# A hybrid decoder step on one core: attention scores as two full 128-row matmuls, and RWKV's triangular inverse with T and A·T side by side in one PSUM bank

## The chip, the cores and the metric

One core of one Trainium2 chip runs the whole program in one launch. The metric is the device time of that launch in microseconds (us). TensorE (PE) does the matmuls, VectorE (DVE), ScalarE (ACT) and GpSimd (POOL) do the elementwise work, and 16 DMA engines move data; every engine works through its own list of instructions in order and waits on semaphores for the others.

## The reference

One layer of a decoder: a combined input projection feeds four groups of heads, whose gated outputs go through one output projection. Two of the groups matter here.

```python
# group A, differential attention: 4 heads, two softmax maps (c) per head, 64 numbers per query and key
s = jnp.einsum('bqhcd,bkhcd->bhcqk', q, k) * (DQK ** -0.5)      # + ALiBi bias, causal
pr = jax.nn.softmax(s + bias)
w = pr[:, :, 0] - lam * pr[:, :, 1]
...
# group B, RWKV-7: 8 heads of 64, 1024 steps, a state s of 64x64 per head
def step(s, inp):
    sa = jnp.einsum('bhvk,bhk->bhv', s, a_t)
    s = s * w_t[:, :, None, :] + sa[..., None] * b_t[:, :, None, :] + v_t[..., None] * k_t[:, :, None, :]
    return s, jnp.einsum('bhvk,bhk->bhv', s, r_t)
```

The kernel computes group B in chunks of 64 steps. Inside a chunk the rows `sa` depend on each other through a strictly triangular 64x64 matrix A, so that each head and chunk needs the triangular inverse T = (I - A)^-1.

## The kernel before

**The projections.** `Kern.block` (line 562) computes x @ w as a stream of matmuls with 128 rows, 128 columns of weights and 344 tokens: each product is made of three fp32r matmuls (high·high, high·low, low·high), as operands are split into a high and a low part (`split_piece`, lines 538 and 539: ACT makes `whi`, DVE `wlo`). There are 9,936 of these and 96 more in `block_dt`; every other stage is woven into this stream.

**The weaving.** `Driver.run` holds generators ("lanes"), each a stage of the model. A lane runs until it yields a number, the microseconds of model time after which it wants to go on; in between the driver emits matmuls of the projection, 8 at a time, and each adds 344/2400 us to the model clock `K.now`. So the order of the work on PE is set by the program, ahead of time, from these numbers; the operations of the small matmuls add to the clock as well (`K.mm`, `K.tp`, and a line in `mixer_a`). The Tile layer then orders each engine's list and adds the semaphores.

**Attention** (`mixer_a`, one head after the other). Keys and queries come from DRAM as `k2` and `q2`: for each map c the 64 rows stand twice, on partitions 0 to 63 and 64 to 127. ACT rounds the keys to fp32r (`kh`) and DVE makes the remainder `kl` on 64 partitions; `qs` holds the rounded queries on 64 partitions and their remainder on the other 64. For each block i of 128 queries and each piece of up to 512 keys, `scores` issues two matmuls per map (lines 1507 and 1508): `qs` x `kh` over 128 rows gives (high + low query)·high key, and `qs` x `kl` over 64 rows adds high query·low key. Then one DVE instruction (line 1511) adds the bias and takes the maximum, ACT does the exponential (line 1518) and DVE normalises (lines 1521, 1522). Scores use a pool of three PSUM banks; the scores of block i + 1 are issued ahead of the transposes `p_wt` and the products `p_o` of block i.

**RWKV** (`Rwkv`, three lanes). `elements` prepares the operands of a unit (2 blocks of two heads, 128 steps: J = 4 matrices for each half of the partitions, 16 units in all), `products` does the matmuls, `norm` the output. For each unit `products` does:

- `p_gram`: 8 matmuls give the 64x64 matrices; ACT copies A to `at` (line 926), DVE masks the rest (`gs`, line 936);
- the inverse by doubling: T starts with blocks of 2 on its diagonal, four levels double them to 32, and a last step joins two of 32. T is kept with its transpose in `tm`. A level l (0 to 3) takes two rounds through PE: `p_w` = A_l · T (8 matmuls of 64 rows, 64 columns, 64 wide), DVE adds the identity (`wpl`, line 949), `p_t` = that times T (8 matmuls); then ACT copies `p_t` to `tm` (line 972) and DVE transposes it (line 973). DVE also masks the next level's A (`nl`, line 963). The last step works on quarters of 32x32 (two `p_w` groups, lines 983 to 991);
- `p_bt`: transposes of `bk`; then for each half c of the unit `p_z`, `p_y` (products with the state S), `p_sa` (T times z), `p_s` and `p_y` (update of the state and output), each ended by small copies on DVE and ACT.

A small f32 matmul shows as two records in the trace; the 8 matmuls of a level are 16 records. `products` yields 0.8 and 0.7 between the two rounds of a level.

Of the kernel before, what the change touches and what calls it, by code (L numbers as in the profile page):

```python
# [45 lines left out]
def constants():  # L46

    p = np.arange(128)
    s = p % 64
    t = np.arange(64)  # L50
    c = {}
    c["ident"] = np.eye(128)
    strict = (t[None, :] > s[:, None])
    incl = (t[None, :] >= s[:, None])
    c["gmask"] = np.concatenate([strict, incl], 1)
    lm = []
    for n in (1, 2, 4, 8, 16):
# [7 lines left out]
    c["mt"] = np.concatenate([x[1] for x in lm[1:]], 1)  # L65
    c["bones"] = (p[:, None] // 64 == p[None, :] // 64)
# [64 lines left out]
class Kern:  # L131
# [46 lines left out]
    def mm(self, out, lhsT, rhs, start, stop):  # L178
# [5 lines left out]
        self.nc.tensor.matmul(out, lhsT=lhsT, rhs=rhs, start=start, stop=stop)  # L184
# [643 lines left out]
class Rwkv:  # L828
# [16 lines left out]
    TWO = ("nl", "tm", "rn", "gst4", "bon128")  # L845
# [56 lines left out]
    def products(self):  # L902
# [7 lines left out]
        for it in range(self.UNITS):  # L910
# [17 lines left out]
            tm = P.tile([128, 2, J, 64], F32, name="tm", tag="tm")  # L928
            nc.vector.tensor_tensor(tm[:, 1], at, m1, op=ALU.mult)
            nc.vector.tensor_tensor(tm[:, 1], tm[:, 1], e64.to_broadcast([128, J, 64]), op=ALU.add)  # L930
            flat = lambda x: x.rearrange("p j t -> p (j t)")
            nc.vector.transpose(flat(tm[:, 0]), flat(tm[:, 1]))  # L932
            nl = P.tile([128, J, 64], F32, name="nl", tag="nl")
            nc.vector.tensor_tensor(nl, at, mt[:, 0].unsqueeze(1).to_broadcast([128, J, 64]), op=ALU.mult)
            for h in range(2):
                nc.vector.tensor_tensor(gs[:, h], pg[h], gm, op=ALU.mult)

            yield 2.3
            sav = P.tile([128, J, 2, 64], F32, name="sav", tag="sav")
            s4 = sav.rearrange("p (b c) h t -> p b c h t", c=2)  # L940
            for l in range(4):
                pw = ps("p_w")
                pwv = pw[:, :J * 64].rearrange("p (j t) -> p j t", j=J)
                for j in range(J):
                    for h in range(2):
                        q = slice(h * 64, h * 64 + 64)
                        K.mm(pwv[q, j, :], lhsT=nl[q, j, :], rhs=tm[q, 0, j, :], start=True, stop=True)
                wp = P.tile([128, J, 64], F32, name="wpl", tag="nl")
                nc.vector.tensor_tensor(wp, pwv, e64.to_broadcast([128, J, 64]), op=ALU.add)  # L949
                if l == 0:  # L950

                    p = ps("p_v")
                    for b in range(nb):
                        K.tp(p[:, b * 128:b * 128 + 128], v[:, b, :], K.id)
                    pv = p[:, :N].rearrange("p (b h t) -> p b h t", b=nb, h=2)
# [15 lines left out]
                tm = P.tile([128, 2, J, 64], F32, name="tm", tag="tm")  # L971
                nc.scalar.copy(tm[:, 0], ptv)  # L972
                nc.vector.transpose(flat(tm[:, 1]), pt[:, :J * 64])  # L973
                yield 0.7
# [3 lines left out]
            wp = P.tile([128, J, 64], F32, name="wpl", tag="nl")  # L978
            for j in range(J):
                for h in range(0, 128, 64):  # L980
                    u, w = slice(h, h + 32), slice(h + 32, h + 64)
                    K.mm(pwv[w, j, 0:32], lhsT=at[u, j, 32:64], rhs=tm[u, 0, j, 0:32], start=True, stop=True)
            nc.vector.tensor_copy(out=wp[32:64, :, 0:32], in_=pwv[32:64, :, 0:32])
            nc.scalar.copy(wp[96:128, :, 0:32], pwv[96:128, :, 0:32])
            yield 1.05
            for j in range(J):
                for h in range(0, 128, 64):
                    u, w = slice(h, h + 32), slice(h + 32, h + 64)
                    K.mm(pwv[u, j, 32:64], lhsT=wp[w, j, 0:32], rhs=tm[w, 1, j, 32:64], start=True, stop=True)
            nc.vector.tensor_copy(out=tm[0:32, 1, :, 32:64], in_=pwv[0:32, :, 32:64])  # L990
            nc.scalar.copy(tm[64:96, 1, :, 32:64], pwv[64:96, :, 32:64])
            tq = tm[:, 1]

            bt = P.tile([128, J, 2, 64], F32, name="bt", tag="tm")
# [8 lines left out]
            for c in range(2):  # L1003

                pz, py = ps("p_z"), ps("p_y")
                bh = [(b, h, slice(h * 64, h * 64 + 64), slice(64 - h * 64, 128 - h * 64), slice(b * 64, b * 64 + 64))
                      for b in range(nb) for h in range(2)]
                for b, h, q, w, n in bh:
                    K.mm(pz[w, n], lhsT=ar[q, 2 * b + c, 0, :], rhs=S[q, b0 + b, :], start=b == 0, stop=False)
                for b, h, q, w, n in bh:  # L1010
                    K.mm(pz[w, n], lhsT=gs[q, h, 2 * b + c, 0:64], rhs=sav[q, 2 * b + c, h, :], start=False, stop=b == nb - 1)
                for b, h, q, w, n in bh:
                    K.mm(py[q, n], lhsT=ar[q, 2 * b + c, 1, :], rhs=S[q, b0 + b, :], start=b == 0, stop=False)
                z = P.tile([128, nb, 64], F32, name="z", tag="z")
                nc.vector.tensor_copy(out=z.rearrange("p b t -> p (b t)"), in_=pz[:, :nb * 64])
                yield 0.51
# [34 lines left out]
        for a in range(2):  # L1051
            so = P.tile([64, 4, 64], F32, name="sob", tag="nl")
# [407 lines left out]
def mixer_a(K, P):  # L1460
    nc = K.nc
    for h in range(4):
# [6 lines left out]
        q2 = P.tile([128, 2, T], F32, name="aq2", tag="ae", bufs=2)  # L1469
# [8 lines left out]
        qs = P.tile([128, 2, T], F32R, name="aqs", tag="aqs")  # L1478
        kh = P.tile([128, 2, T], F32R, name="akh", tag="akh")
        kl = P.tile([128, T], F32R, name="akl", tag="akl")  # L1480
        nc.scalar.copy(kh, k2)
        yield 0.00
        for c in range(2):
            r = slice(c * 64, c * 64 + 64)
            nc.vector.tensor_tensor(kl[r], k2[r, c, :], kh[r, c, :].bitcast(F32), op=ALU.subtract)
        nc.scalar.copy(qs, q2)
        yield 1.50
        for c in range(2):
            r = slice(64 - c * 64, 128 - c * 64)
            nc.vector.tensor_tensor(qs[r, c, :], q2[r, c, :], qs[r, c, :].bitcast(F32), op=ALU.subtract)  # L1490
        yield 1.00
# [4 lines left out]
        def scores(i):  # L1496
# [3 lines left out]
            npc = (nk + 511) // 512  # L1500
            for pc in range(npc):
                k0, k1 = pc * 512, min(nk, pc * 512 + 512)
                for c in range(2):
                    r = slice(c * 64, c * 64 + 64)
                    p = K.ps("p_s", 0)
                    t = slice(i * 128, i * 128 + 128)
                    nc.tensor.matmul(p[:, :k1 - k0], lhsT=qs[:, c, t], rhs=kh[:, c, k0:k1], start=True, stop=False)
                    nc.tensor.matmul(p[:, :k1 - k0], lhsT=qs[r, c, t], rhs=kl[r, k0:k1], start=False, stop=True)  # L1508
                    K.now += 2 * max(k1 - k0, 256) / 2400
# [612 lines left out]
```

## Time and profile before

| | us |
|---|---|
| median of 3 runs (lowest to highest) | 2227.99 (2224.55 to 2231.98) |
| the profiled execution's own time | 2238.66 |
| its span, first to last instruction | 2236.9 |
| attention on PE, about | 176 to 540 |
| RWKV's products on PE, about | 685 to 1396 |
| granted TensorE clock, mean | 0.995 |

A row of the timeline gives the start of an instruction (or of a run of equal ones, with their count), its duration, engine, line, operation, what it writes and reads, and its shape; an idle time ahead of it stands in brackets with what ended it. Matmuls overlap in the pipeline and their ends are modelled: what one costs PE is read from the distance between starts.

### The profile page before, as it was taken

What the parts mean: (1) busy time and instruction counts of PE and PEld (TensorE: products, weight loads), DVE (VectorE), ACT (ScalarE), POOL (GpSimd) and SP (SyncE); (2) the same over time, 40 slices, a digit from 0 to 9 for tenths busy, and PEclk for the clock granted to TensorE, in tenths of its full rate; (3) what the DMA queues carried; (4) which work ended last, traced back from release to release, by engine and by line L of the source; (5) the groups of instructions that cost most, each with busy time, mean ns of one, the idle gap of its engine ahead of it and who ended that gap; (6) DMA issues with size and microseconds to landing.
All of it is one profiled execution on the core that took longest, in us unless ns stands there. A gap on an engine that the chain in (4) does not pass through costs nothing. (4 is left out here: it accounts for less than half of the span.)

```text
span 2236.9 us, 42918 instructions
## 1 busy us (share of the span) xinstructions
PE 2183.9 (98%) x16964; PEld 2010.3 (90%) x16964; DVE 1189.1 (53%) x2869; ACT 813.1 (36%) x2079; POOL 184.9 (8%) x246
## 2 busy tenths in 40 slices
PE   8999999999999999999999999999999999999997
PEld 6798989899998888889888888899989999999997
DVE  6714353444225567673668875476653544333554
ACT  7724343444222344432344343112211134333544
POOL 2100000000000000020100000350031100000000
PEclk9999999999999999999999999999999999999999
DMA  7652425241322223152322211664565584222791
GB/s 262 192 136 61 133 68 142 67 119 41 112 66 63 68 64 86 57 172 76 107 58 81 66 53 49 183 216 129 150 183 144 160 262 130 79 74 72 223 255 51
DMA packets 320851, 263.50 MB, mean 118 GB/s; under 512 B 29356, under 2 KB 294906, under 8 KB 319952
## 3 DMA queue, kind: packets, MB, share of 16 engines
q1 hardware_dynamic: 307792, 218.92, 34.2%
q0 software_dynamic: 12192, 40.28, 5.8%
q8 instruction: 134, 2.20, 0.4%
q10 hardware_dynamic: 664, 1.54, 0.2%
q14 instruction: 69, 0.57, 0.1%
HBM read 205.93 MB, written 54.80 MB: 117 GB/s over the span
## 5 line engine op out<-in xcount | busy, mean ns | idle before, releaser
L562 PE MATMUL acc<-hh,wlo 128*128 128x344 f32 x3312 | 1079.1, 326 | 6.0 <-DVE wlo L539 3.8
L562 PE MATMUL acc<-hh,whi 128*128 128x344 f32 x3312 | 1076.2, 325 | 6.9 <-ACT whi L538 2.6
L562 PE MATMUL acc<-hl,whi 128*128 128x344 f32 x3312 | 1078.0, 325 | 1.6 <-issue 1.6
L562 PEld LDWEIGHTS acc<-hh,whi 128*128 128x128 f32 x3312 | 624.4, 189 | 17.3 <-ACT whi L538 3.6
L562 PEld LDWEIGHTS acc<-hh,wlo 128*128 128x128 f32 x3312 | 623.1, 188 | 17.3 <-DVE wlo L539 5.9
L562 PEld LDWEIGHTS acc<-hl,whi 128*128 128x128 f32 x3312 | 625.8, 189 | 8.8 <-issue 3.6
L539 DVE TENSOR_TENSOR wlo<-raw,whi 128x512 fp32r<-128x512 f32 x300 | 206.9, 690 | 406.9 <-ACT whi L538 398.1
L538 ACT CAST whi<-raw 128x512 fp32r<-128x512 f32 x300 | 185.4, 618 | 494.1 <-PE acc L562 401.1
L1511 DVE CUSTOM_DVE_ANT_0 ae<-p_s,al 128x512 f32<-128x512 f32 (+3 forms) x96 | 52.9, 557 | 51.0 <-PE p_s L1508 49.9
L1518 ACT ACTIVATE ae<-ae,am 128x128 f32<-128x128 f32 (+7 forms) x64 | 49.2, 771 | 57.6 <-DVE am L1515 57.5
L1832 ACT ACTIVATE p_out<-xo 128x128 f32<-128x128 f32 (+1 forms) x144 | 39.8, 276 | 78.5 <-DVE xo L1831 74.1
L1831 DVE TENSOR_TENSOR xo<-xo,p_out 128x128 f32<-128x128 f32 (+1 forms) x144 | 39.4, 280 | 27.1 <-PE p_out L188 26.9
L972 ACT COPY tm<-p_t 128x256 f32<-128x256 f32 x64 | 23.9, 373 | 74.0 <-PE p_t L184 73.8
L184 PEld LDWEIGHTS p_w<-tm,nl 64*64 64x64 f32 x1024 | 34.9, 134 | 17.5 <-issue 12.9
L539 DVE TENSOR_TENSOR wlo<-oraw,whi 128x512 fp32r<-128x512 f32 x48 | 33.2, 692 | 31.7 <-ACT whi L538 31.4
L184 PEld LDWEIGHTS p_t<-wpl,tm 64*64 64x64 f32 x1024 | 35.0, 134 | 15.4 <-issue 8.6
L184 PE MATMUL p_w<-tm,nl 64*64 64x64 f32 x1024 | 43.6, 224 | 2.7 <-DVE tm L932 2.7
L184 PE MATMUL p_t<-wpl,tm 64*64 64x64 f32 x1024 | 43.9, 224 | 0.5 <-DVE wpl L949 0.5
L214 POOL TENSOR_TENSOR ass<-ass,mhalf 128x8 f32<-128x8 f32 x4 | 6.6, 1643 | 453.4 <-DVE ass L1559 453.4
L1619 POOL DMA_INDIRECT sakp<-in_cache_diff_k,sapt x32 | 40.9, 1278 | 31.3 <-DMA r<-sda 16.7
L973 DVE STREAM_TRANSPOSE tm<-p_t 128x256 f32<-128x256 f32 x64 | 28.5, 446 | 26.8 <-ACT tm L972 26.5
L214 POOL TENSOR_TENSOR osr<-osr,mhalf 128x1 f32<-128x1 f32 (+1 forms) x9 | 6.0, 691 | 443.8 <-DMA xo<-in_x_prompt 319.6
(468 smaller groups left out, 2708.2 us busy)
## 6 DMA issues: line engine op xcount, KB each, us to landing
raw<-in_w_in SPq DMA_DIRECT2D x220, 256.0 KB
raw<-in_w_out SPq DMA_DIRECT2D x80, 256.0 KB
oraw<-in_w_out SPq DMA_DIRECT2D x12, 1024.0 KB
evm<-sm SPq DMA_DIRECT2D x48, 172.0 KB
sB<-evs SPq DMA_DIRECT2D x39, 172.0 KB
sA<-evp SPq DMA_DIRECT2D x36, 172.0 KB
evo<-so SPq DMA_DIRECT2D x36, 172.0 KB
sm<-evo SPq DMA_DIRECT2D x36, 172.0 KB
```

What stands on the lines that cost most here:

```text
L184: self.nc.tensor.matmul(out, lhsT=lhsT, rhs=rhs, start=start, stop=stop)
L214: self.nc.gpsimd.tensor_tensor(out, x, self.mhalf[:P, :n], op=ALU.pow)
L538: nc.scalar.copy(hi, raw)
L539: nc.vector.tensor_tensor(lo, raw, hi.bitcast(F32), op=ALU.subtract)
L562: nc.tensor.matmul(acc[g][:, :G], lhsT=x[:, k, :], rhs=y, start=kp == ko[0] and k == 0 and x is hi and y is a, stop=kp == ko[-1] and k == ...
L972: nc.scalar.copy(tm[:, 0], ptv)
L973: nc.vector.transpose(flat(tm[:, 1]), pt[:, :J * 64])
L1511: nc.vector.tensor_tensor_reduce(e[:, c, k0:k1], p[:, :k1 - k0], al[:, x0:x0 + k1 - k0], 1.0, -3e38, ALU.add, ALU.max, m[:, c, pc:pc + 1])
L1518: nc.scalar.activation(e[:, c, :nk], e[:, c, :nk], AF.Exp, bias=m[:, c, 0:1], accum_out=z[:, c:c + 1])
L1619: nc.gpsimd.indirect_dma_start(out=dst, out_offset=None, in_=I[src].rearrange("a p c -> (a p) c"), in_offset=bass.IndirectOffsetOnAxis(ap= ...
L1831: nc.vector.tensor_tensor(xt, xt, q[:n, k * 128:k * 128 + 128], op=ALU.add)
L1832: nc.scalar.activation(q[:n, k * 128:k * 128 + 128], xt, AF.Square, accum_out=self.ss[:n, 3 * g + k, cb:cb + 1])
```

## The change

In **attention**, keys are kept in one tile `km`: the rounded keys on partitions 0 to 63, their remainder on 64 to 127, for both maps. The queries are made block by block (`queries(i)`, two buffers, one block ahead): `qt` holds the rounded query on both halves of the partitions (a = 0) and the remainder on both (a = 1). A score is then two matmuls over 128 rows, high query and low query against `km`. `q2` lies in a buffer of its own (the one `qs` had) and not in the pair of buffers of `e`.

In **RWKV**, one PSUM bank `p_t` holds T and A·T side by side for a unit, 32 columns of each for every 64 rows (within the levels up to 16, T has 32x32 blocks on its diagonal alone). A first round of 8 matmuls writes both; then a level takes one round: DVE masks A·T out of the bank (`xl`, x), transposes it in SBUF, ACT copies the bank to SBUF (`rt`), and 8 matmuls add the level's correction to T and to A·T in the bank itself, without clearing it; the last of the four adds to T alone. The 8 matmuls have 64 columns each as before, as two runs of 32, in the last round one run of 32. T's transpose is made once, at the end (`tm`), and T is spread to 64 columns (`tq`). The first state products (c = 0) are issued directly behind the last round, ahead of the 32x32 steps. `products` yields 1.2 for each level, and before `p_sa` of c = 0 it no longer yields.

```diff
@@ Rwkv.products
+            xl = P.tile([128, 2, J, 64], F32, name="xl", tag="xl")
+            xm, lt = xl[:, 0], xl[:, 1]
+            nc.vector.tensor_tensor(xm, at, m1, op=ALU.mult)
+            nc.vector.tensor_tensor(xm, xm, e64.to_broadcast([128, J, 64]), op=ALU.add)
+            nc.vector.transpose(flat(lt), flat(xm))
+            rt = P.tile([128, 2, J, 32], F32, name="rt", tag="rt")
+            nc.gpsimd.tensor_copy(out=rt[:, 0], in_=K.c("eye32").unsqueeze(1).to_broadcast([128, J, 32]))
+            for h in range(2):
+                for o in (0, 32):
+                    q = slice(64 - h * 64 + o, 96 - h * 64 + o)
+                    nc.scalar.copy(rt[q, 1], pg[h][q, :, o:o + 32])
...
-                        K.mm(pwv[q, j, :], lhsT=nl[q, j, :], rhs=tm[q, 0, j, :], start=True, stop=True)
-                wp = P.tile([128, J, 64], F32, name="wpl", tag="nl")
-                nc.vector.tensor_tensor(wp, pwv, e64.to_broadcast([128, J, 64]), op=ALU.add)
...
-                        K.mm(ptv[q, j, :], lhsT=tm[q, 1, j, :], rhs=wp[q, j, :], start=True, stop=True)
-                tm = P.tile([128, 2, J, 64], F32, name="tm", tag="tm")
-                nc.scalar.copy(tm[:, 0], ptv)
-                nc.vector.transpose(flat(tm[:, 1]), pt[:, :J * 64])
-                yield 0.7
...
+                    K.mm(ptv[q, :, j, :], lhsT=lt[q, j, :], rhs=rt[q, :, j, :], start=j == 0, stop=j == J - 1)
...
+                nc.vector.tensor_tensor(xm.rearrange("p j (k t) -> p j k t", k=2),
+                                        ptv[:, 1].unsqueeze(2).to_broadcast([128, J, 2, 32]),
+                                        mt[:, l].rearrange("p (k t) -> p k t", k=2).unsqueeze(1).to_broadcast([128, J, 2, 32]),
+                                        op=ALU.mult)
+                nc.vector.transpose(flat(lt), flat(xm))
+                rt = P.tile([128, 2, J, 32], F32, name="rt", tag="rt")
+                n = 2 if l < 3 else 1
+                nc.scalar.copy(rt[:, :n].rearrange("p a j t -> p (a j t)"), pt[:, :n * J * 32])
...
+                yield 1.2
+                        K.mm(ptv[q, :n, j, :], lhsT=lt[q, j, :], rhs=rt[q, :n, j, :], start=False, stop=j == J - 1,
+                             skip_group_check=True)
+            first = state_products(0)
+            tm = P.tile([128, J, 32], F32, name="tm", tag="tm")
+            nc.vector.transpose(flat(tm), pt[:, :J * 32])
+            tq = P.tile([128, J, 64], F32, name="tq", tag="tq")
...
+                z, py = state_products(c) if c else first
+                if c:
+                    yield 0.51
@@ mixer_a
+        km = P.tile([128, 2, T], F32R, name="akm", tag="akh")
+        nc.scalar.copy(km, k2)
+        nc.vector.tensor_tensor(km[64:128], k2[64:128], km[64:128].bitcast(F32), op=ALU.subtract)
+        def queries(i):
+            t = slice(i * 128, i * 128 + 128)
+            qt = P.tile([128, 2, 2, 128], F32R, name="aqt", tag="aqt", bufs=2)
+            nc.scalar.copy(qt[:, 0], q2[:, :, t])
+            nc.vector.tensor_tensor(qt[:, 1], q2[:, :, t], qt[:, 0].bitcast(F32), op=ALU.subtract)
+            return qt
...
-                    nc.tensor.matmul(p[:, :k1 - k0], lhsT=qs[:, c, t], rhs=kh[:, c, k0:k1], start=True, stop=False)
-                    nc.tensor.matmul(p[:, :k1 - k0], lhsT=qs[r, c, t], rhs=kl[r, k0:k1], start=False, stop=True)
-                    K.now += 2 * max(k1 - k0, 256) / 2400
+                    for a in range(2):
+                        nc.tensor.matmul(p[:, :k1 - k0], lhsT=qt[:, a, c], rhs=km[:, c, k0:k1], start=a == 0, stop=a == 1)
+                    K.now += 2 * max(k1 - k0, 128) / 2200
```

The order of the instructions shows three places. The first is PE in attention, the scores of query block 6 of the first head: `p_o` is the product of block 4, `p_s` a bank of scores, `ak..` are keys, `aq..` queries, `acc` the projection. Before:

```order
L184 MATMUL p_o_2429<-av_2021,aw_2408 128x128 x5
L1507 MATMUL p_s_2440<-akh_1983,aqs_1982 128x512
L1508 MATMUL p_s_2440<-akl_1984,aqs_1982 128x512
L1507 MATMUL p_s_2444<-akh_1983,aqs_1982 128x512
L1508 MATMUL p_s_2444<-akl_1984,aqs_1982 128x512
L1507 MATMUL p_s_2448<-akh_1983,aqs_1982 128x384
L1508 MATMUL p_s_2448<-akl_1984,aqs_1982 128x384
```

The same place on PE now:

```order
L186 MATMUL p_o_2433<-av_2018,aw_2415 128x128 x5
L1531 MATMUL p_s_2447<-akm_1982,aqt_2373 128x512 x2
L1531 MATMUL p_s_2451<-akm_1982,aqt_2373 128x512 x2
L1531 MATMUL p_s_2455<-akm_1982,aqt_2373 128x384 x2
L564 MATMUL acc1_2106<-hh_12_1_1106,whi_2318 128x344
L1531 MATMUL p_s_2459<-akm_1982,aqt_2373 128x384 x2
```

The scores stand where they stood, two matmuls to a bank; the pair is now of one kind.

The second place is DVE in the levels of unit 13, with work of another lane (`sst`, `stt`: the sampled tokens' state) between. Before (`wpl`, `nl` and the transposed `tm` are the level's, `p_w` and `p_t` PE's banks):

```order
L949 TENSOR_TENSOR wpl_13853<-p_w_13844,cst2_5645 128x256
L963 TENSOR_TENSOR nl_13855<-at_13732,cst2_5645 128x256
L783 TENSOR_TENSOR kk_13878<-rkv_13798,pt_134 128x256
L1177 TENSOR_TENSOR stt_13687<-svv_12982,svec_12979 128x1024
L973 STREAM_TRANSPOSE tm_13875<-p_t_13866 128x256
L1179 TENSOR_TENSOR sst_13686<-sst_13686,stt_13687 128x1024
L949 TENSOR_TENSOR wpl_13898<-p_w_13889,cst2_5645 128x256
```

DVE in the levels now (`xl` is the masked A·T and its transpose):

```order
L979 TENSOR_TENSOR xl_13477<-p_t_13428,cst2_5739 128x256
L1189 TENSOR_TENSOR stt_13284<-sst_13283,svec_13276 128x1024
L983 STREAM_TRANSPOSE xl_13477<-xl_13477 128x256
L794 TENSOR_REDUCE rn_13554<-ksq_13513 128x4
L1191 TENSOR_REDUCE ssa_13285<-stt_13284 128x16
L979 TENSOR_TENSOR xl_13506<-p_t_13428,cst2_5739 128x256
```

A level has two DVE instructions instead of three, both between two visits of PE, and the other lane's instruction can stand between them.

The third place is PE around the first `p_sa` of a unit. Before (`p_w` is the second 32x32 step, `p_z` and `p_y` the first state products, `p_xs` another lane's):

```order
L184 MATMUL p_w<-tm,wpl 32x32 x8
L188 MATMUL p_bt<-cst_129,bk 128x128 x4
L184 MATMUL p_z<-S,ar 64x64 x4
L184 MATMUL p_z<-sav,gs 64x64 x4
L184 MATMUL p_y<-S,ar 64x64 x4
L184 MATMUL p_bon<-ksq,cst_5645 128x256
L184 MATMUL p_xs<-xmk,xq 128x256 x2
L184 MATMUL p_sa<-z,tm 64x64 x4
```

Now, in another unit (`p_kb` and `p_kn` belong to the operands of later work):

```order
L186 MATMUL p_w<-tq,wpl 32x32 x8
L190 MATMUL p_bt<-cst_129,bk 128x128 x4
L190 MATMUL p_kb<-cst_129,rx 128x128 x2
L186 MATMUL p_kn<-ksq,cst_5739 128x32
L186 MATMUL p_sa<-z,tq 64x64 x4
```

The state products no longer stand between the 32x32 step and `p_sa`. Over the whole program the projection's stream on PE consists of 519 unbroken runs before and of 477 now.

More of the change, by code (lines that the diff above doesn't have):

```diff
@@ L65, in constants @@
     c["mt"] = np.concatenate([x[1] for x in lm[1:]], 1)
+    c["own"] = (s[:, None] // 32 == t[None, :] // 32)
+    c["eye32"] = (p[:, None] % 32 == np.arange(32)[None, :])
     c["bones"] = (p[:, None] // 64 == p[None, :] // 64)
@@ L175, in ps, with mm @@
         return (self.p2 if ring else self.pb).tile([128, 512], F32, name=name, tag="mx")
-    def mm(self, out, lhsT, rhs, start, stop):
+    def mm(self, out, lhsT, rhs, start, stop, **k):
         cols = 1
@@ L183, in mm @@
         self.now += max(0.03, cols * f * 4 / 2400)
-        self.nc.tensor.matmul(out, lhsT=lhsT, rhs=rhs, start=start, stop=stop)
+        self.nc.tensor.matmul(out, lhsT=lhsT, rhs=rhs, start=start, stop=stop, **k)
     def tp(self, out, in_, ident):
@@ new lines, in state_products @@
+            def state_products(c):
+                pz, py = ps("p_z"), ps("p_y")
+                for b, h, q, w, n in bh:
+                    K.mm(pz[w, n], lhsT=ar[q, 2 * b + c, 0, :], rhs=S[q, b0 + b, :], start=b == 0, stop=False)
+                for b, h, q, w, n in bh:
+                    K.mm(pz[w, n], lhsT=gs[q, h, 2 * b + c, 0:64], rhs=sav[q, 2 * b + c, h, :], start=False, stop=b == nb - 1)
+                for b, h, q, w, n in bh:
+                    K.mm(py[q, n], lhsT=ar[q, 2 * b + c, 1, :], rhs=S[q, b0 + b, :], start=b == 0, stop=False)
+                z = P.tile([128, nb, 64], F32, name="z", tag="z")
+                nc.vector.tensor_copy(out=z.rearrange("p b t -> p (b t)"), in_=pz[:, :nb * 64])
+                return z, py
@@ new lines, in products @@
+            yield 2.3
+            pt = ps("p_t")
+            ptv = pt[:, :J * 64].rearrange("p (a j t) -> p a j t", a=2, j=J)
+            for j in range(J):
+                for h in range(2):
+                    q = slice(h * 64, h * 64 + 64)
+                    K.mm(ptv[q, :, j, :], lhsT=lt[q, j, :], rhs=rt[q, :, j, :], start=j == 0, stop=j == J - 1)
+            p = ps("p_v")
+            for b in range(nb):
+                K.tp(p[:, b * 128:b * 128 + 128], v[:, b, :], K.id)
+            pv = p[:, :N].rearrange("p (b h t) -> p b h t", b=nb, h=2)
@@ L988, in products @@
                     u, w = slice(h, h + 32), slice(h + 32, h + 64)
[L989 to L994, printed above, removed]
+                    K.mm(pwv[u, j, 32:64], lhsT=wp[w, j, :], rhs=tq[w, j, 32:64], start=True, stop=True)
+            nc.vector.tensor_copy(out=tq[0:32, :, 32:64], in_=pwv[0:32, :, 32:64])
+            nc.scalar.copy(tq[64:96, :, 32:64], pwv[64:96, :, 32:64])
+            bt = P.tile([128, J, 2, 64], F32, name="bt", tag="xl")
             p = ps("p_bt")
@@ L1003, in products @@
             for c in range(2):
[L1005 to L1016, printed above, removed]
+                z, py = state_products(c) if c else first
+                if c:
+                    yield 0.51
                 pz = ps("p_sa")
@@ L1468, in mixer_a @@
         k2 = P.tile([128, 2, T], F32, name="ak2", tag="ae", bufs=2)
-        q2 = P.tile([128, 2, T], F32, name="aq2", tag="ae", bufs=2)
+        q2 = P.tile([128, 2, T], F32, name="aq2", tag="aqs")
         for t, src in ((k2, K.sA[4 + h]), (q2, K.sA[h])):
@@ L1476, in mixer_a @@
         yield 6.0
[L1478 to L1481, printed above, removed]
+        km = P.tile([128, 2, T], F32R, name="akm", tag="akh")
+        nc.scalar.copy(km, k2)
         yield 0.00
[L1483 to L1491, printed above, removed]
+        nc.vector.tensor_tensor(km[64:128], k2[64:128], km[64:128].bitcast(F32), op=ALU.subtract)
+        yield 2.50
+        def queries(i):
[4 more added lines that the diff above has]
+            return qt
+        qts = [queries(0)]
         v = P.tile([128, 8, 128], F32, name="av", tag="av")
@@ L1500, in scores @@
             npc = (nk + 511) // 512
+            qt = qts.pop()
+            if i < 7:
+                qts.append(queries(i + 1))
             for pc in range(npc):
```

47 lines of the change are left out of this document (16 added, 31 removed).

## The prediction

> **What bounds the kernel now.** I read the page first, then PE's waits, then its timeline.
>
> ```profile
> span 2236.9 us, 42918 instructions
> PE 2183.9 (98%) x16964; PEld 2010.3 (90%) x16964; DVE 1189.1 (53%) x2869; ACT 813.1 (36%) x2079; POOL 184.9 (8%) x246
> L562 PE MATMUL acc<-hh,wlo 128*128 128x344 f32 x3312 | 1079.1, 326 | 6.0 <-DVE wlo L539 3.8
> ```
>
> PE is busy 98% of the span, and its costliest line waits 6 us in all. Busy time is no price, though: the three kinds of product, 1079 us each like this one, would not fit into the span one after the other; a record's 326 ns overlap its neighbours'. The price is the step from start to start:
>
> ```profile
> 119.79 0.32 PE L562 MATMUL acc<-hl,whi 128*128 128x344 f32 x1
> ...
> 122.94 0.32 PE L562 MATMUL acc<-hh,whi 128*128 128x344 f32 x1
> ```
>
> PE's waits between 680 and 1396 us, RWKV's stretch, longest first (microseconds in total, times, longest):
>
> ```profile
> PE p_w L184 <- DVE tm L932: 2.7, 2, 1.8
> PE p_yt L188 <- DVE y L1090: 2.1, 2, 1.2
> ```
>
> In the timeline twenty steps take 3.15 us, 0.157 us each. The waits are these two and three smaller ones; in attention's stretch (176 to 560 us) that view is empty. So the kernel lasts as long as PE needs for what is on its list: the projection's 10,032 matmuls can't shrink, and every microsecond that other matmuls take between them stands in the span. The change is priced by the PE time that it takes out, less new waits.
>
> **Attention.** The count of the scores, then from the timeline the first and last matmul of a run for each width:
>
> ```profile
> L1507 PE MATMUL p_s<-akh,aqs x96: 218/442/502, 176.4 to 531.2; 128*128 128x512 f32 x48, 128*128 128x128 f32 x16, 128*128 128x256 f32 x16, 128*128 128x384 f32 x16
> ```
>
> ```profile
> 227.61 1.06 PE L184 MATMUL p_o<-av,aw 128*128 128x128 f32 x8
> 228.42 0.48 PE L1507 MATMUL p_s<-akh,aqs 128*128 128x512 f32 x1
> 228.83 0.50 PE L1508 MATMUL p_s<-akl,aqs 64*128 64x512 f32 x1
> ...
> 231.82 0.42 PE L562 MATMUL acc<-hl,whi 128*128 128x344 f32 x1
> 187.02 0.42 PE L1507 MATMUL p_s<-akh,aqs 128*128 128x384 f32 x1
> ...
> 188.49 0.43 PE L562 MATMUL acc<-hl,whi 128*128 128x344 f32 x1
> 184.31 0.28 PE L1507 MATMUL p_s<-akh,aqs 128*128 128x256 f32 x1
> ...
> 185.46 0.33 PE L188 MATMUL p_wt<-cst,ae 128*128 128x128 f32 x1
> 176.44 0.22 PE L1507 MATMUL p_s<-akh,aqs 128*128 128x128 f32 x1
> ...
> 177.35 0.65 PE L188 MATMUL p_kv<-cst,ak 128*128 128x128 f32 x4
> ```
>
> Four pairs 512 wide take 3.40 us (0.85 a pair); two pairs of 384 take 1.47 (0.735), of 256 1.15 (0.575), of 128 0.91 (0.455). Sum: 48 x 0.85 + 16 x (0.735 + 0.575 + 0.455) = 69.0 us. A pair costs about 0.35 us even before width counts: each step between a 128-row and a 64-row matmul costs some 0.2 us beside the columns. Two 128-row matmuls of the same kind in a row stand elsewhere in the trace:
>
> ```profile
> 58.41 0.40 PE L467 MATMUL macc<-wmh,ml 128*128 128x512 f32 x1
> ...
> 59.35 0.40 PE L468 MATMUL macc<-wml,mh 128*128 128x512 f32 x1
> ```
>
> Four steps in 0.94 us, 0.235 us each for 512 columns, with the same split operands; 344 columns took 0.157. On the line through both, 384 columns give 0.176 and 256 give 0.116; for 128 I take no less than the 0.10 us of the `p_o` row above (8 records in 0.81 us), 0.11. New sum: 48 x 0.47 + 16 x (0.35 + 0.23 + 0.22) = 35.4 us, **33.6 us less** (the ends: nothing, if the old pace belongs to these tiles and not to the mix of heights, and 36).
>
> Some of it comes back. Banks are three, and DVE must read one before the fourth pair of a block may start:
>
> ```profile
> 229.37 0.69 DVE L1511 CUSTOM_DVE_ANT_0 ae<-p_s,al 128x512 f32<-128x512 f32 x1 [1.36 <-PE p_s L1508]
> ```
>
> DVE starts 0.54 us after the pair's second matmul (228.83) and takes 0.69. Now: second matmul at 0.235, DVE done at 1.46, bank free at about 1.55 us; the fourth pair would be due at 1.16 to 1.41 in blocks 4 to 7. That is 0.15 to 0.4 us for 16 blocks, **4 us back**. The busy time of the stretch, engine by engine (length, PE, PEld, DVE, ACT, POOL, clock, DMA):
>
> ```profile
> 176.00:560.00 384.00, 384.00 (x2337) 346.43 (x2336) 167.03 (x450) 160.00 (x389) 6.57 (x4) 1.00 0.33 92
> ```
>
> DVE is busy 167 of 384 us and ACT 160. The work that makes operands (ACT's copies, DVE's subtractions) has the same elements as before in smaller pieces; both engines have room for it beside PE. `q2` in its own buffer only lets loads go earlier.
>
> **RWKV's levels.** The records of the rounds, then from the timeline a round alone between projection matmuls, one of half its records, and one of 32 columns:
>
> ```profile
> L184 PE MATMUL p_t<-wpl,tm 64*64 64x64 f32 x1024 | 43.9, 224 | 0.5 <-DVE wpl L949 0.5
> L184 PE MATMUL p_w<-tm,nl 64*64 64x64 f32 x1024 | 43.6, 224 | 2.7 <-DVE tm L932 2.7
> ```
>
> ```profile
> 688.72 0.32 PE L562 MATMUL acc<-hh,wlo 128*128 128x344 f32 x1
> 688.97 0.68 PE L184 MATMUL p_w<-tm,nl 64*64 64x64 f32 x16
> 689.59 0.43 PE L562 MATMUL acc<-hh,whi 128*128 128x344 f32 x1
> 689.85 0.32 PE L562 MATMUL acc<-hl,whi 128*128 128x344 f32 x1
> 706.79 0.32 PE L562 MATMUL acc<-hh,whi 128*128 128x344 f32 x1
> 707.04 0.45 PE L184 MATMUL p_sa<-z,tm 64*64 64x64 f32 x8
> 707.42 0.43 PE L562 MATMUL acc<-hl,whi 128*128 128x344 f32 x1
> 701.44 0.32 PE L562 MATMUL acc<-hh,wlo 128*128 128x344 f32 x1
> 701.69 0.44 PE L184 MATMUL p_w<-tm,at 32*32 32x32 f32 x16
> 702.06 0.42 PE L562 MATMUL acc<-hh,whi 128*128 128x344 f32 x1
> ```
>
> The round of 16 records puts 0.87 us between two projection matmuls, 0.71 more than 0.157; 8 records put 0.47 more, 16 records of 32 columns 0.46. So a record of 64 columns costs 0.03 us, and going in and out 0.23. Behind a group the next step is also long, 0.26 instead of 0.157 (689.59 to 689.85).
>
> - Removed: 2 x 1024 records are 128 rounds, 128 x 0.71 = 90.9 us.
> - Added: 16 units x 4 full rounds (the first, and three levels) x 0.71 = 45.4 us; the fourth level moves half the columns and stands directly ahead of `p_z`, of the same 64x64 form, so that it shares their way in and out: 16 records x 0.015 = 0.24, 3.8 us in 16 units. The ends: 0, by the row of 32 columns, whose 0.46 is hardly more than the way in and out with records at 0.015, and 7.7 with records at full price.
> - Together **41.7 us less**. The Trainium skill, TensorEngine Tiling (Array Packing), Instruction Overhead, holds that a matmul with one column takes as long as one with 60, so that halving 64 columns would save almost nothing; by it this term would be 3.9 us smaller. The 32-column row speaks against it: its 16 records cost 0.25 us less than 16 of 64 columns, though in a smaller tile.
> - The stream is cut 477 times instead of 519: 42 x 0.10 = **4.2 us less**.
>
> What follows a round on DVE and ACT is off PE, but it is what the next round waits for:
>
> ```profile
> 693.10 0.68 PE L184 MATMUL p_w<-tm,nl 64*64 64x64 f32 x16
> 693.83 0.42 DVE L949 TENSOR_TENSOR wpl<-p_w,cst 128x256 f32<-128x256 f32 x1 [1.21 <-PE p_w L184]
> ```
>
> ```profile
> L973 DVE STREAM_TRANSPOSE tm<-p_t 128x256 f32<-128x256 f32 x64 | 28.5, 446 | 26.8 <-ACT tm L972 26.5
> L972 ACT COPY tm<-p_t 128x256 f32<-128x256 f32 x64 | 23.9, 373 | 74.0 <-PE p_t L184 73.8
> L1183 DVE TENSOR_REDUCE sy<-stt 128x16 f32<-128x1024 f32 x2 | 2.4, 1213 | 0.0
> ```
>
> From a round's start to DVE's start are 0.73 us, then a mask (0.42) and a transpose in SBUF (0.45), with ACT's copy of the same bank (0.37) behind the mask and beside the transpose: about 1.7 us from round to round. One round (0.71) and 8 projection matmuls (8 x 0.157) give 1.97 us of cover, and the yield of 1.2 us is more than one batch's 8 x 344/2400 = 1.15, so that many levels get two batches. Before, `p_t` to `p_w` needed 0.73 + 0.37 + 0.45, as DVE's transpose waited for ACT (26.5 us of the row), under the same batch. Uncovered is a level where DVE holds other work between mask and transpose: the sampled tokens' 1.21 us instructions, as the order shows. I take **5 us of new waits** there and at `p_sa`, where the 32x32 step now has only transposes to hide its copies. POOL's new copy of the identity waits for nothing of the unit; the copies on ACT at the unit's start run while the projection does.
>
> Sum: 33.6 - 4 + 41.7 + 4.2 - 5 = **70.5 us less**. The profiled execution took 2238.66 us (its span and 1.8 us around it), which would become 2168; it lay 10.7 us above the median of the runs, 2227.99, and the saving is in PE's list, the same in any run. Forecast: **2157.5 us**.
>
> **Rivals.**
>
> - *The bank is written in two runs.* A `p_t` matmul writes 32 columns of T and 32 of A·T, 512 bytes apart, and reads `rt` in the same way; no row of before has such an output. If each run cost as a move of its own, a record would gain up to its 0.03 us again: 16 x 64 x 0.03 = 31 us on the 64 full rounds, saving 40, 2188 us. The Trainium skill, PSUM — Partial Sum Buffer, Specifications, says that any non-contiguous access pattern slows matmuls significantly, which is this rival; no run so far shows it. Against it stands that runs of 32 are still many cycles long. Chance 0.08.
> - *The scores don't get faster.* If the 0.2 us beside the columns belongs to the score tiles and not to the mix of 128 and 64 rows, attention gives nothing: saving 41, 2187 us. Against it: every group of another height in RWKV pays the same sort of entry, and `macc` has none. Chance 0.07.
> - *DVE sets the pace of the scores.* The queries of the next block are rounded on ACT and subtracted on DVE in the middle of the scores' own readers. If DVE stands about 1 us behind in the 16 late blocks, 16 us come back: 2174 us. For it: 0.69 us of DVE against 0.47 of PE per pair; against it, the 167 of 384 us above. Chance 0.12.
>
> - *Slower than before.* A level is now one chain of two DVE instructions under one round of cover. Where DVE's queue puts other lanes' work between them, PE stands still with the whole projection behind the waiting matmul. At 79 us gross less 4, the point is 75/80 = 0.94 us of waiting on each of 80 rounds; a 1.21 us instruction ahead of each would give 97 us of waits, 2250 us. For it: DVE is in one line and 53% busy over the span; against it, the waits on DVE's `tm` and `wpl` today are 3.2 us in the two rows. Chance 0.05, of which 0.02 lies near no change.
>
> **How the numbers follow.** The sum as it stands has 0.68: 2157.5 us. Its unknown terms reach from no new waits and a free fourth level (9 + 4 us better, with the runs' spread of 4 us 2140) to the doubled columns and the scores without gain (2188 and 2187, with the spread 2192). So 2140 to 2192 leaves out the slower rival and a doubling of the waits beyond them. A measurement of this kernel tells 0.3%, 6.7 us, from no change. Faster by more: 0.95, within: 0.02, slower: 0.03.
>
> **What would show it.** Right: two scores 512 wide at about 0.24 us from start to start with no 64-row form left; DVE's readers end behind PE's fourth pair, with waits of 0.2 to 0.4 us for a bank in blocks 4 to 7; 64 rounds of `p_t` with 0.71 us between projection matmuls, the fourth level joined to `p_z`; PE's waits in RWKV a few us. Wrong: rounds of `p_t` well over 0.71 without a wait ahead (two runs); score steps still 0.4; waits of PE on `xl` of tens of us (slower).

## The result, and the profile after

| | us |
|---|---|
| changed kernel, median of 4 runs (lowest to highest) | 2168.91 (2165.84 to 2170.23) |
| kernel before, median of 4 runs | 2227.34 (2224.55 to 2231.98) |
| ratio, 95% interval | 0.9734 (0.9714 to 0.9753) |
| profiled execution after: time, span | 2168.77, 2167.0 |

The change makes the kernel 58.4 us faster by medians; 70.5 were forecast. First the page's span and the busy time of the engines in the changed kernel:

```profile
span 2167.0 us, 41564 instructions
PE 2103.3 (97%) x16196; PEld 1977.2 (91%) x16196; DVE 1169.3 (54%) x2857; ACT 829.6 (38%) x2171; POOL 194.2 (9%) x262
```

PE is still busy for 97% of the span. It issues 768 records less, the 128 rounds of 16 less the 80 that came. Attention in the timeline of PE, the last query block of the first head (four pairs 512 wide, then the fourth of them alone), then two pairs 256 wide and two 128 wide:

```profile
221.78 1.50 PE L186 MATMUL p_o<-av,aw 128*128 128x128 f32 x12
223.04 2.23 PE L1531 MATMUL p_s<-akm,aqt 128*128 128x512 f32 x8
224.54 0.73 PE L1531 MATMUL p_s<-akm,aqt 128*128 128x512 f32 x2
225.11 0.32 PE L564 MATMUL acc<-hh,whi 128*128 128x344 f32 x1
225.27 0.32 PE L564 MATMUL acc<-hl,whi 128*128 128x344 f32 x1
...
184.32 0.64 PE L1531 MATMUL p_s<-akm,aqt 128*128 128x256 f32 x4
184.79 0.27 PE L190 MATMUL p_wt<-cst,ae 128*128 128x128 f32 x1
...
176.86 0.56 PE L1531 MATMUL p_s<-akm,aqt 128*128 128x128 f32 x4
177.26 0.62 PE L190 MATMUL p_kv<-cst,ak 128*128 128x128 f32 x4
```

Four wide pairs take 2.07 us where they took 3.40. At 0.47 a pair that would be 1.88. Of the 0.19 us left over some 0.14 are the fourth pair's wait for its bank, which DVE's first reader holds until 223.79 + 0.69 = 224.48: the step into this pair is 0.27 us and the pair itself takes 0.57 (224.54 to 225.11) instead of 0.47. Most of the rest is the first step of the run, 0.31, which other runs of scores behind `p_o` show as well. The wait stands in the last block of each head, four times in all; in the other late blocks the steps between 512-wide matmuls, behind the first, are 0.23 to 0.24 us. The view of waits does not show it, as it lies under the modelled end of the matmul ahead.

```profile
223.79 0.69 DVE L1534 CUSTOM_DVE_ANT_0 ae<-p_s,al 128x512 f32<-128x512 f32 x1 [2.12 <-PE p_s L1531]
```

Pairs of 256 take 0.235 us and of 128 take 0.20, where 0.23 and 0.22 were forecast. Now a level's round alone, and a fourth level joined with the state products (start times on PE):

```profile
655.81 0.32 PE L564 MATMUL acc<-hh,wlo 128*128 128x344 f32 x1
656.06 0.68 PE L186 MATMUL p_t<-rt,xl 64*64 64x64 f32 x16
656.67 0.42 PE L564 MATMUL acc<-hh,whi 128*128 128x344 f32 x1
656.93 0.32 PE L564 MATMUL acc<-hl,whi 128*128 128x344 f32 x1
...
737.86 0.32 PE L564 MATMUL acc<-hh,wlo 128*128 128x344 f32 x1
738.11 0.48 PE L186 MATMUL p_t<-rt,xl 64*64 64x32 f32 x10
...
739.05 0.43 PE L564 MATMUL acc<-hh,whi 128*128 128x344 f32 x1
...
749.64 0.31 PE L564 MATMUL acc<-hh,wlo 128*128 128x344 f32 x1
749.88 0.45 PE L186 MATMUL p_z<-S,ar 64*64 64x64 f32 x8
...
750.55 0.42 PE L564 MATMUL acc<-hh,whi 128*128 128x344 f32 x1
```

The round puts 0.86 us between two projection matmuls, 0.70 more than 0.157, as a round did before. The fourth level with the state products takes 1.19 us, the state products alone (the unit's second half) 0.91: the half-width level costs 0.28, where 0.24 were forecast. By the Trainium skill, TensorEngine Tiling (Array Packing), Instruction Overhead, a matmul with one column has the same latency as one with 60; read as a price in a stream, that would make the half-width level cost nearly a full one's 0.48. The measured 0.28 decides against that reading here.

So the prices of PE's work hold. What is longer than forecast is PE's waits in RWKV's stretch (640 to 1345 us; us in total, times, longest):

```profile
PE p_t L186 <- DVE xl L937: 7.6, 9, 1.6
PE p_t L186 <- DVE xl L983: 6.9, 8, 1.4
```

14.5 us on `xl`, 7.6 of them ahead of the first round of a unit and 6.9 at the levels. A first round in the timeline, PE's and DVE's rows:

```profile
797.73 0.61 PE L186 MATMUL p_gram<-ar,bk 64*128 64x128 f32 x8
...
800.58 0.42 DVE L1112 TENSOR_TENSOR y<-y,gst 128x256 f32<-128x256 f32 x1 [1.12 <-POOL gst L216]
...
800.92 0.42 DVE L935 TENSOR_TENSOR xl<-at,cst 128x256 f32<-128x256 f32 x1
801.26 0.68 DVE L945 TENSOR_TENSOR gs<-p_gram,cst 128x512 f32<-128x512 f32 x1
801.86 0.41 DVE L936 TENSOR_TENSOR xl<-xl,cst 128x256 f32<-128x256 f32 x1
802.19 0.68 DVE L945 TENSOR_TENSOR gs<-p_gram,cst 128x512 f32<-128x512 f32 x1
802.79 0.43 DVE L937 STREAM_TRANSPOSE xl<-xl 128x256 f32<-128x256 f32 x1
803.37 0.68 PE L186 MATMUL p_t<-rt,xl 64*64 64x64 f32 x16 [1.45 <-DVE xl L937]
```

DVE stands 1.12 us for another unit's norm (`y`, waiting for GpSimd), then does mask, sum and transpose of the first `xl` with the two masks `gs` of 0.68 us between them. PE waits 1.45 us for the transpose. The code writes `gs` behind the transpose; on DVE's list it stands between.

### The profile page after: what moved, and what is told of

Read it like the earlier page. It is cut to its first block, busy times and chain, and to the rows that moved or that the text cites. A ratio compares the mean times of both kernels' runs of the same rounds, so it can differ in the third digit from the quotient of the medians.

```text
span 2167.0 us, 41564 instructions
## 1 busy us (share of the span) xinstructions
PE 2103.3 (97%) x16196; PEld 1977.2 (91%) x16196; DVE 1169.3 (54%) x2857; ACT 829.6 (38%) x2171; POOL 194.2 (9%) x262
## 5 line engine op out<-in xcount | busy, mean ns | idle before, releaser
L186 PEld LDWEIGHTS p_t<-rt,xl 64*64 64x64 f32 x1280 | 44.8, 134 | 33.9 <-issue 24.0
L186 PE MATMUL p_t<-rt,xl 64*64 64x64 f32 (+1 forms) x1280 | 55.0, 223 | 15.3 <-DVE xl L937 7.6
L541 DVE TENSOR_TENSOR wlo<-oraw,whi 128x512 fp32r<-128x512 f32 x48 | 33.2, 692 | 31.7 <-ACT whi L540 31.5
L1531 PE MATMUL p_s<-akm,aqt 128*128 128x512 f32 (+3 forms) x192 | 45.3, 360 | 0.0
L1857 DVE TENSOR_TENSOR xo<-xo,fgc 128x128 f32<-128x128 f32 (+1 forms) x96 | 27.0, 288 | 28.7 <-ACT p_out L1855 27.7
L986 ACT COPY rt<-p_t 128x256 f32<-128x256 f32 x64 | 22.0, 344 | 53.2 <-DVE xl L979 48.7
L715 DVE SCALAR_TENSOR_TENSOR evc<-evx,der,evc 128x344 f32<-128x344 f32 (+1 forms) x72 | 40.5, 567 | 3.1 <-ACT evc L713 2.9
L540 ACT CAST whi<-oraw 128x512 fp32r<-128x512 f32 x48 | 29.6, 617 | 32.5 <-PE acc L564 31.2
```

Of the source, the lines that this page charges most:

```text
L540: nc.scalar.copy(hi, raw)
L541: nc.vector.tensor_tensor(lo, raw, hi.bitcast(F32), op=ALU.subtract)
L715: nc.vector.scalar_tensor_tensor(e[:, :n], x[:, t:t + n], w(t), e[:, :n], op0=ALU.mult, op1=ALU.add)
L986: nc.scalar.copy(rt[:, :n].rearrange("p a j t -> p (a j t)"), pt[:, :n * J * 32])
L1531: nc.tensor.matmul(p[:, :k1 - k0], lhsT=qt[:, a, c], rhs=km[:, c, k0:k1], start=a == 0, stop=a == 1)
L1857: nc.vector.tensor_tensor(xt, xt, self.fg(cb)[:n], op=ALU.mult)
```

## The experiments

The kernels ran in three series, the first on one chip, the second and third on another. The kernel before took 2227.25, 2239.98 and 2233.99 us (medians) in the three, so kernels of different series are compared by their ratio to it.

**Series 1: which half is short, and the two prices.** `attn_only` is the kernel before with the diff's hunk of `mixer_a`; `rwkv_only` is the kernel before with all other hunks.

> The kernel before with the attention part of the change alone; RWKV as before. Theory (the shortfall against the forecast lies in RWKV: 14.5 us of PE's waits for the masked tile xl where 5 us were allowed, and the attention term is right): 33.6 - 4 = 30 us less than before, about 2198 us, with score steps of 0.24 us at 512 columns. Rival (the scores gained less than priced, RWKV gained what was said): 2209 us, with waits for banks or steps of 0.3 us in the late query blocks.

Measured: 2195.19 us, ratio 0.9852 (0.9836 to 0.9869), 32.1 us less (29.2 to 36.5). The view of PE's waits in attention is empty. Adding up over the trace what each group of small matmuls with scores in it puts between the projection matmuls on its two sides, less 0.157, gives 87.9 us in 41 groups before and 57.1 here: 30.9 less.

> The kernel before with the RWKV part of the change alone; attention as before. Theory: 41.7 + 4.2 - 15 = 31 us less than before, about 2196 us, with some 15 us of PE's waits on xl between 640 and 1400 us. Rival (attention is short, RWKV gives its 41 us): 2186 us, with few waits on xl.

Measured: 2198.2 us, ratio 0.9868 (0.9851 to 0.9885), 29.0 us less (25.6 to 33.2). The shortfall is RWKV's; the rival falls. PE's waits, the first two rows between 640 and 1400 us:

```profile
PE p_t L186 <- DVE xl L937: 7.3, 9, 1.6
PE p_t L186 <- DVE xl L983: 5.9, 7, 1.4
```

All rows of that view without the projection's own make 19.6 us; in the kernel before they made 6.5. The groups in RWKV's stretch (550 to 1450 us), added up as above, make 288.3 us in 281 groups before and 261.8 in 239 here: 26.5 less, within the interval of the clock. As 13.1 us more of them are waits, the work itself gave 39.6.

`score64` runs the second matmul of a pair over 64 rows, as the kernel before did, with the new tiles:

```diff
+                        r = slice(0, 64) if a else slice(0, 128)
-                        nc.tensor.matmul(p[:, :k1 - k0], lhsT=qt[:, a, c], rhs=km[:, c, k0:k1], start=a == 0, stop=a == 1)
+                        nc.tensor.matmul(p[:, :k1 - k0], lhsT=qt[r, a, c], rhs=km[r, c, k0:k1], start=a == 0, stop=a == 1)
```

> The changed kernel, but the second score matmul (low query) runs over 64 rows, the high key alone; this leaves out only the product of the two low parts, which the kernel before left out too. Columns, tiles, readers and counts stay. Theory (a step between 128 and 64 rows costs some 0.2 us beside the columns): the pair goes back from 0.47 to 0.85 us at 512 columns, 96 pairs take 30 us more, 2199 us. Rival (the old pace belonged to the score tiles or their readers, not to the heights): no change, 2169 us.

Measured: 2200.77 us, ratio 0.9885 (0.9869 to 0.9902), 32 us above the changed kernel. The same four wide pairs on PE:

```profile
230.17 3.48 PE L1532 MATMUL p_s<-akm,aqt 128*128 128x512 f32 x8
233.58 0.43 PE L564 MATMUL acc<-hh,whi 128*128 128x344 f32 x1
233.84 0.32 PE L564 MATMUL acc<-hl,whi 128*128 128x344 f32 x1
```

3.41 us, the 3.40 of the kernel before, with other tiles and operands made differently. So the low query's matmul over 64 rows is what costs, and not the tiles or their readers: that is shown. That it is the change of height, and not 64 rows by themselves, is read from the trace: the step from 128 to 64 rows and the step back are both 0.41 to 0.43 us. No run has two 64-row scores in a row.

`contig` lays T and A·T of a matrix side by side:

```diff
-            ptv = pt[:, :J * 64].rearrange("p (a j t) -> p a j t", a=2, j=J)
+            ptv = pt[:, :J * 64].rearrange("p (j a t) -> p j a t", a=2, j=J)
...
-                        K.mm(ptv[q, :n, j, :], lhsT=lt[q, j, :], rhs=rt[q, :n, j, :], start=False, stop=j == J - 1,
+                        K.mm(ptv[q, j, :n], lhsT=lt[q, j, :], rhs=rt[q, j, :n], start=False, stop=j == J - 1,
...
```

> The changed kernel with the bank p_t and its copy rt laid out so that T and A.T of one matrix lie side by side: each matmul of a level reads and writes 64 columns in one run instead of two runs of 32; DVE and ACT read with strides instead. Theory (two runs cost PE nothing: a round of 16 records takes 0.705 us in the changed kernel's profile, the price of one run before): no change, 2169 us within 4, rounds at 0.70 us. Rival (each run costs as a move of its own): up to 0.03 us on each of 1024 records less, down to 2138 us, rounds at 0.4 us.

Measured: 2165.98 us, ratio 0.9726 (0.9710 to 0.9742), no difference that can be told from the changed kernel. A round on PE:

```profile
660.14 0.32 PE L564 MATMUL acc<-hh,whi 128*128 128x344 f32 x1
660.39 0.68 PE L186 MATMUL p_t<-rt,xl 64*64 64x64 f32 x16
661.00 0.42 PE L564 MATMUL acc<-hl,whi 128*128 128x344 f32 x1
```

0.86 us again, with one run of 64 columns instead of two of 32: two runs cost nothing here. By the Trainium skill, PSUM — Partial Sum Buffer, Specifications, any non-contiguous access pattern slows matmuls significantly. Runs of 32 numbers 512 bytes apart did not here.

**Series 2: can the waits be covered?** Two kernels change `products`' yields only. `yield_first` has the first of these edits, `yield_both` both:

```diff
-            yield 2.3
+            yield 4.6
             pt = ps("p_t")
...
-                yield 1.2
+                yield 2.4
                 for j in range(J):
```

> The changed kernel with the yield ahead of each unit's first round raised from 2.3 to 4.6, so that more projection matmuls stand between p_gram and p_t. Theory (the 7.6 us in 9 waits for the first xl are time in which DVE's mask, sum and transpose, with other lanes' work between them, outlast the cover): these waits fall under 1 us and the time by 7 us, about 2162 us. Rival (PE waits for the unit's chain wherever it is put, so that the waits come back in the levels or at the end of RWKV's lanes): 2169 us or more.

> The changed kernel with 4.6 ahead of the first round and 2.4 instead of 1.2 at each level. Theory: both waits on xl, 14.5 us in the changed kernel's profile, fall under 2 us in all, 2155 us. Rival (longer units make RWKV end later, and lanes that hang on it leave PE less to hide behind, or the groups that stood together come apart): no gain beyond that of the first yield alone, 2162 us, or a loss.

Measured: ratios 0.9735 (0.9712 to 0.9758) and 0.9750 (0.9730 to 0.9771) to the kernel before, against 0.9734 of the changed kernel: no gain. The waits did go (1.3 us on `xl` are left in each). The windows before and behind 1360 us (length, busy time and count of PE, PEld, DVE, ACT, POOL, then clock, DMA share and GB/s) of a second profile of the changed kernel (`after_again`, series 3), then of `yield_both`:

```profile
640.00:1360.00 720.00, 697.09 (x6993) 613.82 (x6993) 475.29 (x1246) 290.44 (x834) 71.77 (x118) 1.00 0.29 81
1360.00:2176.00 816.00, 782.25 (x5193) 768.48 (x5191) 413.82 (x884) 255.57 (x679) 92.97 (x96) 0.98 0.53 155
```

```profile
640.00:1360.00 720.00, 713.53 (x7135) 632.57 (x7134) 473.88 (x1234) 292.86 (x836) 63.88 (x112) 1.00 0.30 82
1360.00:2177.00 817.00, 762.98 (x5058) 747.69 (x5056) 415.03 (x898) 254.09 (x678) 92.22 (x101) 0.98 0.53 154
```

Between 640 and 1360 us `yield_both` issues 142 matmuls more; of the projection alone it has 153 more done by 1360, 24 us at 0.157. Behind 1360 it has 135 fewer to do and takes as long. The rows say where the time went: PE's idle time (length less busy time) falls from 22.9 to 6.5 us ahead of 1360 and grows from 33.8 to 54.0 behind it. Where PE stands there, in the timeline around 1776 us:

```profile
1771.38 0.65 PE L564 MATMUL acc<-hh,whi 128*128 128x344 f32 x1 [8.00 <-DVE evg L751]
1771.83 0.49 PE L564 MATMUL acc<-hl,whi 128*128 128x344 f32 x1
...
1773.04 1.75 SPq L748 DMA_DIRECT2D evo<-so  x2
...
1774.70 0.49 PE L564 MATMUL acc<-hh,wlo 128*128 128x344 f32 x1
1780.87 0.52 DVE L752 SCALAR_TENSOR_TENSOR evo<-evg,evo 128x344 f32<-128x344 f32 x1 [9.54 <-DMA evo<-so]
...
1781.87 0.66 PE L564 MATMUL acc<-hh,whi 128*128 128x344 f32 x1 [6.68 <-DVE evg L751]
```

At the second of these waits the gate's reader of an accumulator (`evg`) stands on DVE behind a product (`evo`) that waits 9.54 us for its load, and the projection stands behind the accumulator. The rival holds: what PE gains in RWKV it loses behind it. Such a wait costs more than its own length: behind the first, PE's steps are 0.287 us instead of 0.157 (ten from 1771.83 to 1774.70), with a granted clock of 0.50 from 1771.3 to 1775 us.

`late_q` moves the call of `queries(i + 1)` behind the loop over the pieces:

```diff
-            if i < 7:
-                qts.append(queries(i + 1))
             for pc in range(npc):
...
+            if i < 7:
+                qts.append(queries(i + 1))
             if npc == 2:
```

> The changed kernel, but the queries of block i + 1 are rounded and subtracted behind the scores' readers of block i and not ahead of them. Theory (DVE reads the banks in time; PE's list sets attention's time): 2169 us within 4, and PE's waits in attention stay empty. Rival (the subtraction ahead of the readers holds a bank, some 0.2 us a block): 28 blocks, 6 us faster, 2163 us.

Measured: ratio 0.9726 (0.9702 to 0.9750), not to be told from the changed kernel; attention's waits are one row of 0.2 us. That fits the theory, but the 6 us of the rival lie inside the interval, so the time alone does not decide. The trace does: the 41 groups with scores add up to 57.1 us as in the changed kernel, so nothing was won at the banks.

`before_again` is the kernel before, unchanged.

> The kernel before, unchanged, profiled once more. Theory (the shown profile of before lies 10.7 us above its median by stalls of that one execution, such as those in the projection's stream at 1443 to 1454 and at 1734 us): a time within 4 us of 2227, steps of the same size in every group, and fewer such stalls. Rival (the profiled execution is always slower than the others): about 2238 us again.

Measured: 2237.71 us, one execution, in a series where the kernel before has a median of 2239.98 (2233.15 to 2243.62). On this chip such a time is the ordinary one, so neither expectation is met: it is not near 2227, and the profiled execution is no slower than the others. Steps over 0.6 us in the projection's stream make 12.9 us here and 15.9 in the first profile, most of them at 1451 to 1466 us; they differ by 3 us, so they do not account for the 10.7. The chip of the first profile is not on record, and why that profile lies above its median stays open.

**Series 3: is a wait a cost?** `after_again` is the changed kernel, unchanged. `first_free` takes the dependence on A away by leaving the 2x2 blocks of A out of T; the instructions stay:

```diff
-            nc.vector.tensor_tensor(xm, at, m1, op=ALU.mult)
+            nc.vector.tensor_tensor(xm, e64.to_broadcast([128, J, 64]), m1, op=ALU.mult)
```

> The changed kernel, unchanged, beside the three that follow and on their chip. Theory and rival alike: 0.973 of the kernel before, with 14 us of PE's waits on xl. It is what the other three are compared with.

> The changed kernel, but the first xl of a unit is made from two constants instead of A and a constant; the 2x2 blocks of A are left out of T, all instructions stay, and the first round no longer hangs on ACT's copy of A and the mask behind it. Theory (a wait of PE on a lane costs the program its length): the 7.6 us of waits on the first xl go and the time falls by 6 to 8 us, to 0.970 of before. Rival (what PE gains there is lost again where the projection waits for readers and loads near the end, as with the longer yields): the waits go and the time stays at 0.973.

Measured: `after_again` 2177.11 us, 0.9736 (0.9717 to 0.9755); `first_free` 2174.91 us, 0.9731 (0.9709 to 0.9753). PE's waits on `xl`, of `after_again` and then of `first_free`:

```profile
PE p_t L186 <- DVE xl L937: 7.7, 9, 1.6
PE p_t L186 <- DVE xl L983: 4.7, 6, 1.4
```

```profile
PE p_t L186 <- DVE xl L983: 7.2, 9, 2.2
PE p_t L186 <- DVE xl L937: 2.2, 2, 1.2
```

5.5 us went at the first round, 2.5 came back at the levels: 3 us net, and the medians differ by 2.2, less than the intervals' half width (5 us). It fits neither theory well: the waits were not removed enough to test the price.

`yield_short` changes both yields; `yield_mid` only the first, to 3.4.

```diff
-            yield 2.3
+            yield 1.2
             pt = ps("p_t")
...
-                yield 1.2
+                yield 0.6
                 for j in range(J):
```

> The changed kernel with half the yields: 1.2 ahead of the first round, 0.6 at each level, so that one batch of 8 projection matmuls lies between two rounds and two ahead of the first. Theory (cover is what the yields are for; a level's 1.7 us from round to round leaves 0.3 us under 1.97 us of cover only where DVE is free): waits on xl grow from 14.5 to 40 us or more, the time grows by as much, 2194 us, 0.985 of before. Rival (a unit that ends sooner gives the projection's matmuls back to the end of the program): waits grow and the time grows by less than half of that, under 2182 us, 0.979 of before.

> The changed kernel with 3.4 instead of 2.3 ahead of the first round, one batch of projection matmuls more. Theory (about half of the 7.6 us of waits goes, and so little is shifted that nothing comes back at the end): 4 us less than the changed kernel, 0.972 of before. Rival (each batch spent on the first round is missed behind 1380 us): no change or slower than it.

Measured: `yield_short` 2190.8 us, 0.9816 (0.9790 to 0.9841), 14 us above `after_again`; `yield_mid` 2177.45 us, 0.9739 (0.9720 to 0.9757), no change. Both theories on `yield_short` expected more waits on `xl`. They are fewer, 9.0 us against 12.4 in `after_again`:

```profile
PE p_t L186 <- DVE xl L937: 7.8, 11, 1.7
...
PE p_t L186 <- DVE xl L983: 1.2, 4, 0.4
```

With the half yield a typical 6 projection matmuls stand between two rounds (8 or 16 in the changed kernel): 0.71 + 6 x 0.157 = 1.65 us, the 1.7 that a level needs. The loss is elsewhere: 493 groups cut the projection instead of 476, and all groups together put 456.0 us on PE against 442.4. Of these 13.6 us, 10.8 are idle time of PE inside the groups, 6.4 of that behind 1400 us. Why these waits come was not tried further. For `yield_mid` the rival fits, though the theory's 0.972 lies at the edge of the interval. No version tried beats the changed kernel by more than can be measured.

## Why the prediction was right in kind and 12 us too large

- **Attention**, 33.6 - 4 = 29.6 us forecast, 32.1 (29.2 to 36.5) measured alone. The price of the 64-row matmul is shown by `score64`. From start to start the 96 pairs take 68.4 us before and 38.1 now, where 69.0 and 35.4 + 4 were forecast. That the net is so close is in part luck: the bank's wait is some 0.14 us in 4 blocks, 0.6 us in all and not 4, while the pairs without it take 2 us more than priced. The rivals that scores do not get faster or that DVE sets their pace are refuted: DVE's readers of the four banks follow one another, but PE only waits for the first.
- **RWKV's rounds**, 41.7 us forecast, 39.6 by the trace of `rwkv_only`. The rival of the two runs is refuted by `contig`.
- **New waits**, 5 us forecast, 13.1 in `rwkv_only`: this is the step that failed, by 8 us. The prediction worked out a level's chain (1.7 us under 1.97 of cover) and put the waits only where the sampled tokens' work stood between mask and transpose. It put the first round at nothing, taking ACT's copies at the unit's start as hidden by the projection: there the chain is ACT's copy, mask, sum and transpose, DVE's list put two 0.68 us masks between them, and another unit's norm can stand ahead. Over half of the waits on `xl` are there (7.3 us in `rwkv_only`, against 5.9 at the levels).
- **Fewer cuts**, 4.2 us forecast, 4.1 by the trace of `rwkv_only`. The steps directly behind a group hold 49.9 and 50.1 us beyond 0.157 in the two profiles of the kernel before, 45.8 in `rwkv_only`, 47.0 in `attn_only`, and 43.1 and 43.3 in the two of the changed kernel. The 3 us in `attn_only` were not forecast: behind a 128-row score the projection's next step is 0.16 us (225.11 to 225.27), behind a 64-row one 0.26 (233.58 to 233.84 in `score64`). All other steps over 0.2 us vary between profiles of one kernel by more than the term (24.4 and 18.7 us before, 17.1 and 24.5 now), so that the term is lost in a sum over all long steps.
- **Sum**: RWKV 29.0 instead of 40.9, attention 32.1 instead of 29.6; 61.1 for the two halves alone, 58.4 together, within their intervals. By the terms of the trace RWKV gave 39.6 + 4.1 - 13.1 = 30.6 and attention 30.9 + 3.0 = 33.9, each within its interval. So of the 12 us that RWKV falls short of its forecast the waits account for 8 and the rounds for 2; what is left is less than the measurement can tell. The two profiled executions differ by 69.9 us, nearly the forecast, but the one before lies 11 us above its median and the one after at its own; that agreement is chance. Taking the saving off the median was right.
- **The slower rival** needed 0.94 us of waiting on each of 80 rounds; 14.5 us on 80 rounds are 0.18.

What stays open: the waits explain the shortfall in the account of the trace, but no kernel here turned their removal into time. Longer yields removed them and lost as much behind 1360 us; `first_free` only shifted them. That the program would be shorter by the 13.1 us without the waits is argued, not shown. Whether shorter work on DVE ahead of the first round (without `gs` between) would be a gain was not tried.

## What to carry to other kernels

Price a small matmul between large ones by the distance of starts on both sides of its group, and look whether its height differs from its neighbours': two matmuls of 128 rows instead of one of 128 and one of 64 saved 0.33 us a pair of 512 columns though they move as many. When a change shortens PE's work in a chain of PE and DVE, read the chain's other links at every place where it starts anew, with what the engine's list puts between them, not only in its steady step. And where a static order gives cover to one stage, count what is left for the last one: there the same matmuls may be missed.

## What the runs showed of the hardware

- Adding into a PSUM bank that DVE and ACT read between the rounds cost PE nothing: a round of 16 records takes 0.70 us, as the rounds of the kernel before did, each of which started its bank afresh.
- The projection's steps sometimes stretch to 1 or 2 us where GpSimd issues indirect loads, and the profile names no engine as releaser. In `yield_mid`, on PE:

```profile
1419.54 0.49 PE L564 MATMUL acc<-hh,whi 128*128 128x344 f32 x1 [1.10 <-issue]
...
1421.62 0.45 PE L564 MATMUL acc<-hl,whi 128*128 128x344 f32 x1 [1.59 <-issue]
```

The kernel before has such steps at 1445 to 1452 us, five of them between 0.7 and 1.2 us. That the loads are the cause was not tried.
